# Two residual layers of 512 tokens: modulation loads two steps ahead, x merged tile by tile, and the gating layer's closing product in five pieces

## The chip, the core and the metric

One core of a Trainium2 chip runs one program. The metric is the device time of one execution in microseconds (us). The engines are TensorE (PE: matrix products into PSUM), VectorE (DVE), ScalarE (ACT), GpSimd (POOL) and SyncE (SP), whose queue issues nearly all DMA transfers. Each engine takes its instructions in its own order and waits on semaphores.

## What is computed

A sequence of 512 tokens with 1024 channels goes through two layers. In each layer a token mixer and a dense MLP follow one another, both normalised and modulated by a conditioning vector c, with gates on the way back into x:

```
mod = silu(c) @ ada_w[i] + ada_b[i]          # six vectors of 1024: sh1, sc1, g1, sh2, sc2, g2
h = rms_norm(x, norm_mix[i]) * (1 + sc1) + sh1
x = x + g1 * mixer(h)                        # layer 0: chunked attention, layer 1: spatial gating
h = rms_norm(x, norm_ffn[i]) * (1 + sc2) + sh2
x = x + g2 * (relu(h @ ffn_w1[i]) ** 2 @ ffn_w2[i])

spatial gating: u, v = split(gelu(h @ w_in))         # 3072 columns each
                (u * (W_s rms_norm(v) + b)) @ w_out  # w_out: 3072 x 1024
```

## The kernel before

Everything is float32. Each operand of a product is split into a rounded part (a ScalarE copy) and a rest (a VectorE subtraction), and each product is three TensorE products. Tokens lie in four tiles of 128 rows (t = 0 to 3). On-chip memory is 49 buffers of 4 KB per partition (`NSLOT`), handed out first in, first out by `SL`; a new tile waits until the last user of its buffer is done. The order of instructions on each engine is planned ahead by a list scheduler with a cost model, from the program's order and the dependences. Between `in_order()` and `any_order()` TensorE's order is the written one. `tc.issue_after(ins)` ties what is issued inside it, on the engine of `ins`, behind `ins`.

**Modulation.** For each of the 12 modulation vectors the 1024 x 1024 matrix is read in eight loads of 512 KB; each is multiplied by a column of silu(c) and added up on VectorE (`ada_acc`, L204 and L206), and then either transposed into columns (`ada_columns`) or, for the gates, spread over all rows (`ada_rows`, which also loads the bias row). So a vector is nine steps: one load and its sum each, and a closing one. Ten vectors wait in the queue `bgq` as 90 steps; `bg(n)` takes n of them at set places of the other stages. A step issues its load and uses it at once.

**Layer 0.** Attention head by head; then `ffn(0)`. The MLP's hidden blocks (8 blocks of 512 columns) are "up" steps; each quarter of the second product ("down") is seven block products over sums and differences of blocks (`seven`, Strassen's scheme), which are interleaved with the ups by `steps += [u] + downs[i - 1:i]`. `Run` loads six steps ahead and splits operands three steps ahead. A `Sum` gathers the results (`put`, L489). The last quarter is done plainly by `project_last`: tile by tile, two column halves of 512 each, with the row norm of a finished tile (`rows`) and the transposes of the tile before it (`cols`) in between. x itself has been stored to DRAM (`xs`); `merge(t)` reloads it and computes y * g + x (L798, L799) before the tile's last products are added by `add_residual` (L404: product with the gate, L405: addition to x).

**Layer 1.** The gating half v: two column blocks directly (`gate_tile`, with `bg`), four by the seven-product scheme. Then six column blocks of u (`u_block`), each of four tiles: product, gelu, the gating product, transposes and the split into operands `aTs`. The closing product with `w_out` is cut along the column blocks: `b_down([0])` after block 1, `b_down([1])` after block 2, and after block 5 `b_down([2, 3])` and, in written order, `b_down([4, 5])`. All but the last go through `project`, which multiplies each result with the gate and adds it to x, reloaded whole after block 1. Then `ffn(1)`.

In the functions printed here, those lines matter most: 191 to 209 (step), 266 to 270 (`bg`), 407 to 452 (`project`, `project_last`), 763 to 812 (the steps of the MLP and its end) and 1412 to 1441.

Of the kernel before, what the change touches and what calls it, by code (L numbers as in the profile page):

```python
# [9 lines left out]
F32 = mybir.dt.float32  # L10
# [3 lines left out]
ALU = mybir.AluOpType  # L14
# [38 lines left out]
def trunk_kernel(  # L53
# [37 lines left out]
    def bank():  # L91
        return PS.get([P, 512], F32)
# [82 lines left out]
    def raw_tile(shape):  # L175

        t, i = SL.get(shape, F32)
        return t, lambda: SL.free(i)
# [6 lines left out]
    def ada_acc(l, ms, c0, n, box):  # L185


        nm = len(ms)
        kl = D // n // nm

        def step(k0):
            if k0 == 0:
                box["acc"], box["id"] = SL.get([P, nm * n], F32)
            acc = box["acc"]
            raw, done = raw_tile([P, kl, nm * n])
            src = ada_w[l].rearrange("(p k) (m j) -> p k m j", p=P, m=6)[:, k0:k0 + kl, ms[0]:ms[-1] + 1, c0:c0 + n]
            for k in range(kl if nm > 1 else 0):
                SP.dma_start(raw[:, k, :].rearrange("p (m j) -> p m j", m=nm), src[:, k])
            if nm == 1:
                SP.dma_start(raw, src[:, :, 0, :])  # L200
            for k in range(k0, k0 + kl):
                r, ck = raw[:, k - k0, :], cs[:, k:k + 1]
                if k == 0:
                    V.tensor_scalar(acc, r, ck, None, ALU.mult)  # L204
                else:
                    V.scalar_tensor_tensor(acc, r, ck, acc, ALU.mult, ALU.add)  # L206
            done()

        return [lambda k=k: step(k) for k in range(0, KD, kl)]

    def ada_columns(l, m, box):

# [15 lines left out]
                V.tensor_tensor(r, r, vecT[:, gcol:gcol + 4], ALU.mult)  # L228
        SL.free(box["id"])

    def ada_rows(l, m, box):

        acc = box["acc"]
        raw, done = raw_tile([P, D])
        SP.dma_start(
            raw,
            bass.AP(tensor=ada_b.tensor, offset=ada_b.offset + l * 6 * D + m * D, ap=[[0, P], [1, D]]),
        )
        gt, gi = SL.get([P, D], F32)
        (ah, i0), (al, i1) = SL.get([P, D], F32R), SL.get([P, D], F32R)  # L240
        A.copy(ah, acc)
        V.tensor_tensor(al, acc, f32(ah), ALU.subtract)
        SL.free(i0, i1)
        for hf in range(2):
            sl = slice(hf * 512, hf * 512 + 512)
            ps, pi = bank()
            mm(ps, ones, ah[:, sl], True, False)
            mm(ps, ones, al[:, sl], False, True)
            V.tensor_tensor(gt[:, sl], ps, raw[:, sl], ALU.add)
            PS.free(pi)  # L250
        done()
        gbc[l, m] = (gt, gi)
        SL.free(box["id"])

    def ada_mod(l, m):
        box = {}
        end = (lambda: ada_rows(l, m, box)) if m in (2, 5) else (lambda: ada_columns(l, m, box))
        return ada_acc(l, (m,), 0, D, box) + [end]

    mark = [None]  # L260
# [1 line left out]
    def behind():  # L262

        return tc.issue_after(mark[0].ins) if mark[0] is not None else nullcontext()

    def bg(n):
        with behind():
            for _ in range(n):
                if bgq:
                    bgq.popleft()()  # L270

    region = []

# [130 lines left out]
        V.tensor_tensor(tt, ps, g[:, sl], ALU.mult)  # L404
        V.tensor_tensor(xt[t][:, sl], xt[t][:, sl], tt, ALU.add)  # L405

    def project(actT, src, g):
        for hf in range(2):
            w, ids = wload(src[:, hf * 512:hf * 512 + 512], len(actT))
            for t in range(NT):  # L410
                ps, pi = bank()
                gemm_tok(actT, w, t, ps)
                add_residual(t, hf * 512, ps, g)
                PS.free(pi)
            SL.free(*ids)

    ahead = {}

    def store(t, c0, n):
# [2 lines left out]
    def project_last(actT, src, g, rows, cols=None, after=None, merge=None, spent=None):  # L422


        n = len(actT)
        ws = [wload(src[:, hf * 512:hf * 512 + 512], n) for hf in range(2)]
        if after is not None:
            ahead["w"] = after()
        for t in range(NT):
            if merge is not None:  # L430
                merge(t)
            for hf in range(2):
                w = ws[hf][0]
                nc_ = 256 if cols is None and (t, hf) == (NT - 1, 1) else 512
                for c0 in range(0, 512, nc_):
                    ps, pi = bank()
                    if hf == 1 and t > 0 and cols is not None:
                        gemm_tok(actT, w[:n // 2], t, ps, 0, n - 1)
                        cols(t - 1)
                        gemm_tok(actT, w[n // 2:], t, ps, n // 2, n - 1)  # L440
                    else:
                        gemm_tok(actT, w, t, ps[:, 0:nc_], part=slice(c0, c0 + nc_))
                    add_residual(t, hf * 512 + c0, ps[:, 0:nc_], g)
                    PS.free(pi)
                    if cols is None:
                        store(t, hf * 512 + c0, nc_)
                if t == NT - 1:
                    SL.free(*ws[hf][1])
            if spent is not None:
                spent(t)  # L450
            if cols is not None:
                rows(t)
# [25 lines left out]
    class Sum:  # L478


        def __init__(self):
            self.y, self.ids, self.seen = {}, {}, set()

        def put(self, t, hf, ps):
            if t not in self.y:
# [8 lines left out]
    class Spent:  # L494
# [33 lines left out]
        def done(self, m):  # L528
            self.op.pop(m).free()
# [166 lines left out]
    def ffn(l, norm, rows, cols, after, bgn):  # L696
# [65 lines left out]
        steps = []  # L762
        for q in range(3):
            ups, downs = up_steps(2 * q + 2) + up_steps(2 * q + 3), down_steps(q)
            for i, u in enumerate(ups):
                steps += [u] + downs[i - 1:i]
        run = Run(steps, 3, 3)
        for hf in range(2):
            rng = slice(hf * 256, hf * 256 + 256)
# [20 lines left out]
        up_done(1)  # L790
        run.go()
        g = gbc[l, 5][0]
        def merge(t):

            xt[t], xid[t] = y.y[t], y.ids[t]
            raw, done = raw_tile([P, D])
            SP.dma_start(raw, xs[t])
            V.tensor_tensor(xt[t], xt[t], g, ALU.mult)  # L798
            V.tensor_tensor(xt[t], xt[t], raw, ALU.add)  # L799
            done()  # L800

        in_order()
        parts = {b: Split(t, [P, 4, 256]) for b, (t, _) in quarters(3).items()}
        for b in (6, 7):
# [2 lines left out]
        def spent(t):  # L807
            if t % 2:
                for j in range(2):
                    parts[t // 2, j].free()  # L810

        project_last(plain(parts), ffn_w2[l][3072:4096, :], g, rows, cols, after, merge, spent)


# [86 lines left out]
    def stage_load(ci):  # L901
        c0, k0 = ci * cw, ci * nk
        box = {}
        if ci == 0:
            shift_first(cw)
        for f in ada_acc(0, (1,) if ci == 0 else (0, 1), c0, cw, box):
            f()
        w, ids = wload(a_w_in[0][:, 0:512], nk, k0)
        first_ids.extend(ids)
        w2 = wload_half(a_w_in[0][:, 512:768], k0, nk, V)  # L910
        state[ci] = box, w, w2
# [368 lines left out]
    def gate_tile(cb, t, w):  # L1280

        if cb not in vv:
            vv[cb] = [SL.get([P, 2, 512], F32) for _ in range(2)]
        ps, pi = bank()
        gemm_tok(kept.rows(), w, t, ps)
        bg(((0, 0, 1, 1), (1, 2, 2, 2))[cb][t])
        dst = vv[cb][t // 2][0][:, t % 2, :]
        A.activation(dst, ps, AF.Gelu)
        PS.free(pi)
        tt = tp.tile([P, 512], F32, tag="tt", name="vq")  # L1290
        A.activation(tt, dst, AF.Square, accum_out=vss[:, t, cb:cb + 1])
# [10 lines left out]
    def gate_rows(t):  # L1302
        norm.rows(t)
        if t == 2:
            with tc.issue_after(normed[0].ins):
                kept.half(0)

    ffn(0, mid, gate_rows, norm.cols, lambda: gate_load(0), [3] * 9)
    close(0, 5)
    xs = dp.tile([NT, P, D], F32, name="xsg")  # L1310
    for t in range(NT):
        SP.dma_start(xs[t], xt[t])
        SL.free(xid[t])
    ws = [ahead.pop("w")]
    for t in range(2):
        gate_tile(0, t, ws[0][0])
# [40 lines left out]
    V.tensor_scalar(vr, rsqrt_m2(vs4, NT, SGH), -0.5, None, ALU.mult)  # L1357

    aTs = {}

    def u_block(cb):
        w, ids = u_ahead.pop() if u_ahead else wload(b_w_in[0][:, cb * 512:(cb + 1) * 512], KD)
# [5 lines left out]
        for t in range(NT):  # L1368
# [33 lines left out]
                V.tensor_tensor(lo[:, :, cols], src, f32(hi[:, :, cols]), ALU.subtract)  # L1402
            PS.free(pi)
            SL.free(ui)
            bg((0, 0, 1, 1, 1, 2)[cb])
        SL.free(*ids)
        SL.free(*[i for _, i in vv[cb]])
        aTs[cb] = (tiles, tids)

    last = Norm(1, 3)  # L1410

    def b_down(blocks):
        tiles = [p for b in blocks for p in aTs[b][0]]
        src = b_w_out[0][blocks[0] * 512:(blocks[-1] + 1) * 512, :]
        if 5 in blocks:
            in_order()
            project_last(split_of(tiles), src, gbc[1, 2][0], last.rows, last.cols, lambda: up_ahead(1))
        else:
            project(split_of(tiles), src, gbc[1, 2][0])
        for b in blocks:  # L1420
            for i, j in aTs[b][1]:
                SL.free(i, j)

    u_block(0)
    u_block(1)
    for t in range(NT):
        xt[t], xid[t] = SL.get([P, D], F32)
        SP.dma_start(xt[t], xs[t])
    b_down([0])
    u_block(2)  # L1430
    b_down([1])
    u_block(3)
    u_block(4)
    u_block(5)
    kept.free()
    SL.free(*[i for _, i in wsT])
    b_down([2, 3])
    b_down([4, 5])
    close(1, 2)

    ffn(1, last, None, None, None, [1] * 11)
    any_order()

# [29 lines left out]
```

## Time and profile before

| | |
|---|---|
| median of 3 runs | 1446.78 us (1440.88 to 1448.47) |
| the profiled execution | 1446.44 us |
| its span, first to last instruction | 1444.7 us |
| TensorE products (PE) busy | 1394.3 us, 97% of the span |
| TensorE weight loads (PEld) | 1192.4 us, 83% |
| VectorE (DVE) | 1028.9 us, 71% |
| ScalarE (ACT) | 703.5 us, 49% |
| DMA | 208.92 MB, mean 145 GB/s |

A busy share is an average over stages. Idle time of an engine in a stretch, and what ended it, is read from the stretches and waits further down. PEclk there is the clock granted to TensorE, as a share of 2.4 GHz.

### The profile page before, as it was taken

The numbers are of one execution on the slowest core, as the hardware profiler recorded it, in microseconds if no ns is written. First come the engines' busy times: TensorE is split into PE (matmuls) and PEld (weight loads), VectorE is DVE, ScalarE is ACT, GpSimd is POOL, SyncE is SP. The second block draws the span as 40 slices with busy tenths as digits, with TensorE's granted clock in tenths as the row PEclk, the third lists the DMA queues.
The fourth block names the chain that finished last, engine by engine and source line by source line (L and its number), as shares of the span: only waits on it lengthen the run. The fifth ranks groups of instructions, "written<-read, shape, count | busy, mean of one in ns | idle before, by whom it ended". The sixth has DMA issues, their size and how long they took to land.

```text
span 1444.7 us, 18877 instructions
## 1 busy us (share of the span) xinstructions
PE 1394.3 (97%) x7186; PEld 1192.4 (83%) x7186; DVE 1028.9 (71%) x1509; ACT 703.5 (49%) x1220; POOL 11.1 (1%) x34
## 2 busy tenths in 40 slices
PE   6989889899999999999999999999999999999998
PEld 5879889779888888878878888887889988888877
DVE  6677899667667878865697656868567476867772
ACT  4436667655454544546477532334236355454520
POOL 0000000000000000000000000000000000000000
PEclk9999999899999999999999999999999999999999
DMA  9736664556145263236332343346326225243141
GB/s 332 243 120 174 199 179 129 180 183 227 59 160 190 88 221 103 97 134 231 134 117 88 110 138 123 111 151 206 131 103 247 74 73 160 89 131 102 44 151 53
DMA packets 95458, 208.92 MB, mean 145 GB/s; under 512 B 7808, under 2 KB 25608, under 8 KB 95368
## 3 DMA queue, kind: packets, MB, share of 16 engines
q1 hardware_dynamic: 95184, 207.66, 44.1%
q8 instruction: 56, 0.92, 0.3%
q14 instruction: 34, 0.28, 0.1%
q10 hardware_dynamic: 184, 0.07, 0.0%
HBM read 190.92 MB, written 8.39 MB: 138 GB/s over the span
## 4 chain that ended last, share of the span: by engine, by line
PE 85%; DMA 7%; DVE 5%; ACT 2%; issue 1%; SPq 0%; ACTq 0%; DVEq 0%
PE p L95 81%; DMA s<-in_ada_w 3%; DMA s<-in_ffn_w 1%; DMA s<-in_a_w_in 1%; DVE s L386 1%; DVE s L206 1%; DVE s L473 1%; PE p L1396 1%; ACT s L385 1%; PE p L1092 1%; PE p L312 0%; PE p L1003 0%; DMA vecs<-in_norm_ffn 0%; DMA s<-in_b_w_out 0%; DMA s<-in_x 0%
## 5 line engine op out<-in xcount | busy, mean ns | idle before, releaser
L95 PE MATMUL p<-s,s 128*128 128x512 f32 (+2 forms) x6568 | 1335.5, 363 | 26.4 <-DVE s L473 6.3
L95 PEld LDWEIGHTS p<-s,s 128*128 128x128 f32 x6568 | 1118.2, 191 | 216.1 <-DVE s L473 7.6
L473 DVE TENSOR_TENSOR s<-s,s 128x1024 fp32r<-128x1024 f32 x234 | 281.6, 1221 | 104.8 <-ACT s L472 48.3
L472 ACT CAST s<-s 128x1024 fp32r<-128x1024 f32 x234 | 241.0, 1050 | 180.4 <-PE p L95 99.0
L385 ACT CAST s<-s 128x1024 fp32r<-128x1024 f32 x102 | 106.2, 1050 | 145.1 <-DMA s<-in_b_w_in 30.8
L386 DVE TENSOR_TENSOR s<-s,s 128x1024 fp32r<-128x1024 f32 x102 | 123.6, 1221 | 61.5 <-ACT s L385 55.2
L206 DVE SCALAR_TENSOR_TENSOR s<-s,cs,s 128x1024 f32<-128x1024 f32 (+2 forms) x98 | 108.8, 1110 | 41.4 <-DMA s<-in_ada_w 40.3
L603 DVE TENSOR_TENSOR s<-s,s 128x1024 f32<-128x1024 f32 x64 | 77.7, 1221 | 23.7 <-DMA s<-in_ffn_w 23.1
L711 ACT ACTIVATE r<-p 128x512 f32<-128x512 f32 x64 | 38.1, 595 | 96.7 <-PE p L95 96.6
L404 DVE TENSOR_TENSOR tr<-p,s 128x512 f32<-128x512 f32 (+1 forms) x57 | 38.3, 678 | 54.5 <-PE p L95 54.5
L489 DVE TENSOR_TENSOR s<-p,s 128x512 f32<-128x512 f32 x80 | 54.2, 686 | 18.6 <-PE p L95 18.0
L717 ACT ACTIVATE s<-r 128x256 f32<-128x256 f32 (+1 forms) x112 | 44.9, 442 | 1.0
L301 ACT ACTIVATE s<-s 128x512 f32<-128x512 f32 x32 | 20.2, 631 | 40.7 <-DVE s L405 36.6
L405 DVE TENSOR_TENSOR s<-s,tr 128x512 f32<-128x512 f32 (+1 forms) x57 | 38.4, 680 | 1.1
L1059 ACT ACTIVATE s<-s,nm 128x384 f32<-128x384 f32 (+3 forms) x64 | 35.7, 559 | 6.6 <-DVE nm L1054 4.8
L1054 DVE CUSTOM_DVE_ANT_0 s<-p,s 128x384 f32<-128x384 f32 (+3 forms) x64 | 28.8, 485 | 8.3 <-PE p L95 8.1
L502 DVE TENSOR_TENSOR s<-s,s 128x1024 f32<-128x1024 f32 x28 | 33.5, 1218 | 0.1
L1373 ACT ACTIVATE s<-p 128x512 f32<-128x512 f32 x24 | 14.4, 599 | 39.2 <-PE p L95 38.9
L1401 ACT CAST s<-p 128x256 fp32r<-128x256 f32 x48 | 17.4, 372 | 28.2 <-PE p L1396 22.9
L1402 DVE TENSOR_TENSOR s<-p,s 128x256 fp32r<-128x256 f32 x48 | 19.9, 419 | 14.5 <-ACT s L1401 14.4
L1097 DVE TENSOR_TENSOR s<-p,s 128x512 fp32r<-128x512 f32 (+3 forms) x64 | 29.2, 483 | 0.9 <-ACT s L1096 0.8
L1096 ACT CAST s<-p 128x512 fp32r<-128x512 f32 (+3 forms) x64 | 24.9, 430 | 9.6 <-PE p L1092 9.3
(129 smaller groups left out, 661.0 us busy)
## 6 DMA issues: line engine op xcount, KB each, us to landing
s<-in_ffn_w SPq DMA_DIRECT2D x128, 512.0 KB, 4.4
s<-in_ada_w SPq DMA_DIRECT2D x84, 512.0 KB, 5.0
s<-in_b_w_in SPq DMA_DIRECT2D x48, 512.0 KB, 4.6
s<-in_b_w_out SPq DMA_DIRECT2D x24, 512.0 KB, 5.0
s<-in_a_w_in SPq DMA_DIRECT2D x22, 512.0 KB, 6.1
s<-s SPq DMA_DIRECT2D x64, 128.0 KB, 3.3
s<-in_ada_w SPq DMA_DIRECT2D x24, 256.0 KB, 6.6
s<-in_x SPq DMA_DIRECT2D x8, 512.0 KB, 6.3
```

Of the source, the lines that this page charges most:

```text
L95: T.matmul(ps, lhsT, rhs, start=start, stop=stop, skip_group_check=more)
L206: V.scalar_tensor_tensor(acc, r, ck, acc, ALU.mult, ALU.add)
L385: A.copy(hi, raw)
L386: engs[len(ids) // 2 % len(engs)].tensor_tensor(lo, raw, f32(hi), ALU.subtract)
L404: V.tensor_tensor(tt, ps, g[:, sl], ALU.mult)
L405: V.tensor_tensor(xt[t][:, sl], xt[t][:, sl], tt, ALU.add)
L472: A.copy(self.hi, raw)
L473: mark[0] = V.tensor_tensor(self.lo, raw, f32(self.hi), ALU.subtract)
L489: V.tensor_tensor(dst, ps, dst, ALU.add)
L603: V.tensor_tensor(x[0], y_[0], z[0], ALU.subtract)
L711: A.activation(r, ps, AF.Relu)
L717: A.activation(d, v, AF.Square)
```

## The change

- A modulation step becomes a pair, load and use. `bg` keeps `lead` loads in flight ahead of the use (0 in the attention stage, 2 from layer 0's MLP on) and never takes the queue below `keep`, a limit set for each stage. The gate tiles take one step each and the last of them two; the column blocks 1 to 5 take one per tile. A load's buffer is taken before that of the sum.
- The merge of x moves into `Sum`. Merge of tile 0 is issued right after the operand splits of the last quarter and tied behind the last of them; those of the later tiles are tied behind the row norm last issued. The gating layer uses the same merge: its pieces are summed ungated in a `Sum`, and x is reloaded tile by tile at the end.
- The closing product is in five pieces, [0], [1], [2], [3], [4, 5], with pieces 0 to 3 after column blocks 1 to 4. The first half of the last piece's weights is loaded at the second tile of column block 5.
- In the third quarter of each MLP the downs come one step later.

```diff
-        def step(k0):
-            if k0 == 0:
-                box["acc"], box["id"] = SL.get([P, nm * n], F32)
-            acc = box["acc"]
-            raw, done = raw_tile([P, kl, nm * n])
+        def load(k0):
+            box[k0] = raw, done = raw_tile([P, kl, nm * n])
...
+        def use(k0):
+            if k0 == 0:
+                box["acc"], box["id"] = SL.get([P, nm * n], F32)
+            acc = box["acc"]
+            raw, done = box.pop(k0)
...
+    bgl = deque()
+    lead, keep = [0], [63]
+
     def bg(n):
-        with behind():
-            for _ in range(n):
-                if bgq:
-                    bgq.popleft()()
+        for _ in range(min(n, len(bgl) + len(bgq) - keep[0])):
+            while len(bgq) > keep[0] and len(bgl) <= lead[0]:
+                load, use = bgq.popleft()
+                load()
+                bgl.append(use)
+            with behind():
+                bgl.popleft()()
...
-        ws = [wload(src[:, hf * 512:hf * 512 + 512], n) for hf in range(2)]
+        ws = [ahead.pop(hf) if hf in ahead else wload(src[:, hf * 512:hf * 512 + 512], n) for hf in range(2)]
...
             if merge is not None:
-                merge(t)
+                with tc.issue_after(normed[0].ins) if t else nullcontext():
+                    merge(t)
...
+        def merge(self, xs, g):          # in Sum
+            merged = set()
+            def merge(t):
+                if t in merged:
+                    return
+                merged.add(t)
+                xt[t], xid[t] = self.y[t], self.ids[t]
+                raw, done = raw_tile([P, D])
+                SP.dma_start(raw, xs[t])
+                V.tensor_tensor(xt[t], xt[t], g, ALU.mult)
+                V.tensor_tensor(xt[t], xt[t], raw, ALU.add)
+                done()
+            return merge
...
+            late = 2 if q == 2 else 1
             for i, u in enumerate(ups):
-                steps += [u] + downs[i - 1:i]
+                steps += [u] + (downs[i - late:i - late + 1] if i >= late else [])
+            steps += downs[8 - late:]
...
+        with tc.issue_after(mark[0].ins):          # in ffn, after the operand splits
+            merge = y.merge(xs, g)
+            merge(0)
         project_last(plain(parts), ffn_w2[l][3072:4096, :], g, rows, cols, after, merge, spent)
...
-        bg(((0, 0, 1, 1), (1, 2, 2, 2))[cb][t])
+        bg(1 + ((cb, t) == (1, 3)))
...
+    lead[0], keep[0] = 2, 36
     ffn(0, mid, gate_rows, norm.cols, lambda: gate_load(0), [3] * 9)
...
+    keep[0] = 27          # before the gate tiles; 9 before the column blocks, 0 before ffn(1)
...
-            bg((0, 0, 1, 1, 1, 2)[cb])
+            bg(1 if cb else 0)
+            if (cb, t) == (5, 1):
+                ahead[0] = wload(b_w_out[0][2048:3072, 0:512], KD)
...
-            project_last(split_of(tiles), src, gbc[1, 2][0], last.rows, last.cols, lambda: up_ahead(1))
+            g = gbc[1, 2][0]
+            project_last(split_of(tiles), src, g, last.rows, last.cols, lambda: up_ahead(1), y.merge(xs, g))
         else:
-            project(split_of(tiles), src, gbc[1, 2][0])
+            act = split_of(tiles)
+            for hf in range(2):
+                w, ids = wload(src[:, hf * 512:hf * 512 + 512], len(act))
+                for t in range(NT):
+                    ps, pi = bank()
+                    gemm_tok(act, w, t, ps)
+                    y.put(t, hf, ps)
+                    PS.free(pi)
+                SL.free(*ids)
...
-    for t in range(NT):
-        xt[t], xid[t] = SL.get([P, D], F32)
-        SP.dma_start(xt[t], xs[t])
     b_down([0])
     u_block(2)
     b_down([1])
     u_block(3)
+    b_down([2])
     u_block(4)
+    b_down([3])
     u_block(5)
...
-    b_down([2, 3])
     b_down([4, 5])
```

## Rows read from the trace of the kernel before

**Rows 1.** Stretches: length, busy us by engine, granted clock, DMA share, GB/s.

```profile
core 0: us, PE busy (x) PEld busy (x) DVE busy (x) ACT busy (x) POOL busy (x), PEclk, DMA share, GB/s
100.00:341.00 241.00, 224.03 (x1523) 205.24 (x1522) 190.05 (x449) 152.30 (x354) 8.74 (x21) 0.96 0.61 187
341.00:626.00 285.00, 285.00 (x1405) 242.17 (x1404) 221.52 (x222) 144.04 (x203) 0.00 (x0) 1.00 0.41 134
626.00:642.00 16.00, 12.59 (x49) 9.89 (x48) 13.98 (x15) 4.45 (x7) 0.00 (x0) 0.89 0.26 91
742.00:1004.00 262.00, 262.00 (x1262) 219.63 (x1261) 187.31 (x276) 118.34 (x201) 0.61 (x2) 1.00 0.40 131
...
420.00:440.00 20.00, 20.00 (x90) 16.57 (x89) 13.30 (x13) 13.26 (x18) 0.00 (x0) 1.00 0.77 265
```

**Rows 2.** TensorE's waits, 341 to 1445 us: total, times, longest, us.

```profile
PE p L95 <- DVE s L473: 6.3, 3, 3.4
PE p L95 <- ACT s L385: 2.1, 1, 2.1
PE p L95 <- ACT s L472: 1.4, 1, 1.4
```

**Rows 3.** Timeline of the first gating products: start, duration, engine, idle before.

```profile
709.65 2.60 DVE L206 SCALAR_TENSOR_TENSOR s<-s,cs,s 128x1024 f32<-128x1024 f32 x2 [11.51 <-DMA s<-in_ada_w]
...
735.38 25.00 PE L95 MATMUL p<-s,s 128*128 128x512 f32 x109 [0.98 <-DVE s L473]
```

**Rows 4.** Windows of 2 us behind two of the stops, as rows 1.

```profile
630.00:632.00 2.00, 1.88 (x7) 1.56 (x8) 2.00 (x4) 2.00 (x3) 0.00 (x0) 0.87 0.68 253
632.00:634.00 2.00, 2.00 (x6) 1.51 (x6) 2.00 (x3) 0.52 (x1) 0.00 (x0) 0.50 0.00 0
634.00:636.00 2.00, 2.00 (x9) 1.60 (x8) 2.00 (x3) 0.00 (x0) 0.00 (x0) 0.78 0.00 0
...
1010.00:1012.00 2.00, 2.00 (x8) 1.38 (x7) 2.00 (x5) 0.00 (x0) 0.00 (x0) 0.59 0.91 297
1012.00:1014.00 2.00, 2.00 (x6) 1.53 (x6) 1.18 (x2) 1.26 (x3) 0.00 (x0) 0.56 1.05 392
```

**Rows 5.** Timeline at the end of layer 0's MLP.

```profile
621.64 0.59 ACT L711 ACTIVATE r<-p 128x512 f32<-128x512 f32 x1
...
625.44 1.23 DVE L799 TENSOR_TENSOR s<-s,s 128x1024 f32<-128x1024 f32 x1 [0.41 <-DMA s<-xs]
626.58 1.22 DVE L798 TENSOR_TENSOR s<-s,s 128x1024 f32<-128x1024 f32 x1
...
628.85 1.22 DVE L473 TENSOR_TENSOR s<-s,s 128x1024 fp32r<-128x1024 f32 x1
```

**Rows 6.** Timeline at the end of layer 1's MLP.

```profile
1397.29 1.22 DVE L799 TENSOR_TENSOR s<-s,s 128x1024 f32<-128x1024 f32 x1
1398.42 2.35 DVE L473 TENSOR_TENSOR s<-s,s 128x1024 fp32r<-128x1024 f32 x2
```

**Rows 7.** The page's groups: busy us, mean ns of one, idle before.

```profile
L385 ACT CAST s<-s 128x1024 fp32r<-128x1024 f32 x102 | 106.2, 1050 | 145.1 <-DMA s<-in_b_w_in 30.8
L404 DVE TENSOR_TENSOR tr<-p,s 128x512 f32<-128x512 f32 (+1 forms) x57 | 38.3, 678 | 54.5 <-PE p L95 54.5
L489 DVE TENSOR_TENSOR s<-p,s 128x512 f32<-128x512 f32 x80 | 54.2, 686 | 18.6 <-PE p L95 18.0
```

**Rows 8.** Timeline at the end of the last column block.

```profile
1005.95 1.10 PE L95 MATMUL p<-s,s 128*128 128x128 f32 x6
...
1007.70 0.59 ACT L1373 ACTIVATE s<-p 128x512 f32<-128x512 f32 x1
...
1009.40 0.87 DVE L1391 SCALAR_TENSOR_TENSOR s<-p,bsT,s 128x128 f32<-128x128 f32 x2
```

**Rows 9.** The page's DMA issues: count, size, us to landing.

```profile
s<-in_b_w_out SPq DMA_DIRECT2D x24, 512.0 KB, 5.0
```

**Rows 10.** Waits of SP's queue, 341 to 700 us: total, times, longest, us.

```profile
SPq L684 <- PE p L95: 74.2, 9, 20.2
```

More of the change, by code (lines that the diff above doesn't have):

```diff
@@ L207, in step @@
             done()
-        return [lambda k=k: step(k) for k in range(0, KD, kl)]
+        return [(lambda k=k: load(k), lambda k=k: use(k)) for k in range(0, KD, kl)]
     def ada_columns(l, m, box):
@@ L229, in ada_columns, with ada_bias @@
         SL.free(box["id"])
-    def ada_rows(l, m, box):
-        acc = box["acc"]
-        raw, done = raw_tile([P, D])
+    def ada_bias(l, m, box):
+        box["bias"] = raw, done = raw_tile([P, D])
         SP.dma_start(
@@ L238, in ada_rows @@
         )
+    def ada_rows(l, m, box):
+        acc = box["acc"]
+        raw, done = box["bias"]
         gt, gi = SL.get([P, D], F32)
@@ L256, in ada_mod @@
         box = {}
-        end = (lambda: ada_rows(l, m, box)) if m in (2, 5) else (lambda: ada_columns(l, m, box))
+        if m in (2, 5):
+            end = (lambda: ada_bias(l, m, box), lambda: ada_rows(l, m, box))
+        else:
+            end = (lambda: None, lambda: ada_columns(l, m, box))
         return ada_acc(l, (m,), 0, D, box) + [end]
@@ L405, in add_residual @@
         V.tensor_tensor(xt[t][:, sl], xt[t][:, sl], tt, ALU.add)
-    def project(actT, src, g):
-        for hf in range(2):
-            w, ids = wload(src[:, hf * 512:hf * 512 + 512], len(actT))
-            for t in range(NT):
[L411 to L415, printed above, removed]
     ahead = {}
@@ L792, in ffn @@
         g = gbc[l, 5][0]
[L793 to L800, printed above, removed]
         in_order()
@@ L905, in stage_load @@
             shift_first(cw)
-        for f in ada_acc(0, (1,) if ci == 0 else (0, 1), c0, cw, box):
-            f()
+        for load, use in ada_acc(0, (1,) if ci == 0 else (0, 1), c0, cw, box):
+            load()
+            use()
         w, ids = wload(a_w_in[0][:, 0:512], nk, k0)
@@ L1359, in trunk_kernel @@
     aTs = {}
+    keep[0] = 9
     def u_block(cb):
@@ L1410, in trunk_kernel @@
     last = Norm(1, 3)
+    y = Sum()
     def b_down(blocks):
@@ L1425, in trunk_kernel @@
     u_block(1)
-    for t in range(NT):
-        xt[t], xid[t] = SL.get([P, D], F32)
-        SP.dma_start(xt[t], xs[t])
     b_down([0])
@@ L1436, in trunk_kernel @@
     SL.free(*[i for _, i in wsT])
-    b_down([2, 3])
     b_down([4, 5])
     close(1, 2)
+    keep[0] = 0
     ffn(1, last, None, None, None, [1] * 11)
```

## Prediction

> **What bounds the kernel now.** Read first the stretches of time, then TensorE's waits, then the order on the engine it waits for. The stretches show where a gain can lie: from 341 us on TensorE is busy without a gap in [rows 1] 341 to 626 and 742 to 1004 (285.00 of 285.00, 262.00 of 262.00), and every tensor product there runs at one pace, 90 matmuls in 20 us, 0.222 us each. The number of matmuls doesn't change, so these stretches can only stay or get worse. TensorE's waits from 341 us to the end are three rows [rows 2], 6.3 + 2.1 + 1.4 = 9.8 us, at four places that belong to four handovers:
>
> - a: layer 0's MLP to its closing product, 3.4 us, for VectorE;
> - b: the gating layer's first products, 1.4 + 0.98 = 2.4 us, for ScalarE and VectorE [rows 2, 3];
> - c: the end of its last column block, 2.1 us, for a weight cast;
> - d: layer 1's MLP to its closing product, 6.3 - 3.4 - 0.98 = 1.9 us.
>
> Behind two of them the clock costs more. After stop a the granted clock falls to 0.50, that is from 2.4 to 1.2 GHz; the missing shares in the three windows from 630 us are 0.13 + 0.50 + 0.22 = 0.85 of 2 us, 1.7 us [rows 4]. After stop c they are 0.41 + 0.44 = 0.85, again 1.7 us. So a costs 5.1, b 2.4, c 3.8, d 1.9: 13.2 us are all that this change can take from the time after 341 us. The profiled execution took 1446.44 us (span 1444.7, 1.7 around it), 0.3 below the median 1446.78; the sum is made against 1446.4.
>
> **The change part by part.**
>
> *Merge moved behind the operand splits, third quarter's products one step later (a, d).* In a, VectorE runs in order, and two merge operations (L799, then L798, 1.22 us each) and a weight split stand before the split L473 that TensorE needs [rows 5]. ScalarE took up the last hidden block at 621.64, so its operands could have been split by about 626; the split came at 628.85. In the changed kernel merge(0) is tied behind the four operand splits, and merge(1) to merge(3) behind the row norm before them. Also, two products of 24 matmuls instead of one follow the last hidden block: 24 x 0.222 = 5.3 us more cover. The stop was 3.4, so even with VectorE's old order the cover is longer: a goes whole, 5.1. What is late next is the second half's weights; the same loads as now, split before 624 us, so nothing. In d the row norm is an old one, so merge(1) to merge(3) aren't held there, and one L799 may still stand before the splits as it does now at 1397.29 [rows 6]; but 5.3 us of cover stand against 1.9. I leave 0.5 of 1.9. The step itself moves no work out: the same instructions in another order.
>
> *Modulation loads two steps ahead (b).* Before stop b VectorE stood still 11.51 us for a modulation transfer, and only then started its L206 at 709.65 [rows 3]; nine modulation steps then fall together with the splits of the two big gating products, until TensorE waits. Now one step goes with each of the eight gate tiles and one more with the last, loaded two ahead. Six of L206 at 1.3 us are then done before 709, 7.8 us of VectorE work against a stop of 2.4. The ends: all of the 2.4 gone, or, if the first load of the stage still waits for a free buffer (the stage begins with none in flight, since the limits drain the lead at each boundary), nothing gained. I take 0.8 left, near the lower end, because the idle time is five times the stop. In layer 0's MLP the same edit takes waits from VectorE, but TensorE has none there: worth nothing.
>
> *Bias row loaded as a step of its own, buffer of a load taken before that of the sum.* The instructions are the same. In the attention stage (100 to 341 us, TensorE 224.03 of 241 us, the only other stretch with room) the number of steps at each call is unchanged (27 in all) and the lead is zero, so only the numbers of two buffers change places. Bounds: one like wait of this stage gained or lost, for which stop a's 3.4 is the nearest row; I take 0 and keep +-3.
>
> *Closing product in five pieces, summed ungated (c).* Pieces 2 and 3 were one product behind the last column block; now each stands between blocks. VectorE loses work: 24 results times two operations (L404, and L405 like it, 0.69 each) become 32: 8 copies on ScalarE and 24 additions like L489 at 0.69 [rows 7]. That is 33.1 against 16.6 us, and in front of the last product stand four merges of 2 x 1.22, 9.8 us. Net 6.7 us less, but VectorE isn't the bound between 742 and 1004, so that is worth nothing. What matters is the last block's end. Before, its tail and the missing weights met; now no free product is left to cover the tail, since the closing one runs in written order. The tail: after the last product come gelu 0.59 and the multiply 0.87, against 1.10 us of six gating matmuls [rows 8]: 0.4 us bare, some 0.5 with handovers. The first half's weights are loaded from the second tile of that block on, with two tiles (about 15 us by the pace) still to go: ready. Of the second half, the last two of four loads need buffers that come free only at the tail's end, T. The first of them is ready at T + 5.0 (landing) + 1.05 + 1.22 = T + 7.3 [rows 7, 9], the next at T + 8.5; TensorE wants them after 24 + 12 matmuls, T + 8.0, and 6 matmuls later, T + 9.3. It fits by 0.7; SP issues in order, and the next MLP's four loads stand near: I take 1.0 late. So 1.5 of c is left, too short for a clock drop like the one after 2.1. Ends: 0.5, or rival 1.
>
> *Merges in front of the gating layer's residual.* New work of 2.44 us per tile behind the previous tile's row norm. Queued behind a waiting merge are the residual additions and the norm of that tile, then TensorE's transposes in the middle of the next tile's second half. A tile gives TensorE 48 x 0.222 = 10.7 us; squares, norm, merge and residual take some 7. Ends 0 and 2.44 for the one tile without a predecessor's cover; I take 1.0.
>
> **Sum:** removed 5.1 + 2.4 + 3.8 + 1.9 = 13.2; left 0 + 0.8 + 1.5 + 0.5 = 2.8; new 1.0. Gain 9.4: 1446.4 - 9.4 = 1437.0.
>
> **Rivals.**
>
> 1. *The second half's weights come late at c.* If their transfers queue behind the next MLP's four (392 GB/s after stop c [rows 4], so 512 KB each take 1.3 us), they land 5.3 later; less the margin 0.7 the stop is 4.6, with the clock 6.3, where the forecast has 1.5. For it: these loads stood under pieces 2 and 3 (192 matmuls x 0.222 = 42.6 us), which have moved. Against: they come first in the program. Time: 1437.0 + 4.8 = 1441.8, within 0.5% of before.
>
> 2. *Slower: too few buffers in layer 0's MLP.* Two modulation tiles more are held through the whole of it, of 49 buffers that a count of the code finds nearly all in use. SP is in order and already waits there for buffers [rows 10] (74.2 us for TensorE's releases at the MLP's own weights); a modulation load that waits for one holds the weights behind it. The Trainium skill (Perfetto Trace Analysis, Optimization Strategy) says that a gap that repeats on the engine that should be saturated can mean that the next tile finds no room. By that rule the 341 to 626 stretch, now without a gap, would get one at each of its nine rounds of modulation; no run here shows it yet. A round that starves TensorE costs what a did, 5.1 with the clock. Two use up the gain; from the fourth it is slower by over 0.5%: 1437.0 + 4 x 5.1 = 1457. Against it: some six buffers come free in each 5.3 us step, so two fewer delay a load by about 2 us, and operands are split three steps, 16 us, ahead.
>
> 3. *Nothing:* the stops move instead of going (the written order and a changed plan of VectorE put other splits last). Time 1446. For it: at each stop VectorE is busy nearly throughout the wait (13.98 of 16 us at a). Against: the extra 5.3 us of cover at a and d hold for any order.
>
> **How the numbers follow.** A measurement of this kernel can tell about 0.5%, 7.2 us: the border is 1439.6 and 1454.0. Forecast 0.60 (its own range 1432 to 1442, with the attention stage's +-3), rival 1 0.20, rival 2 0.14, rival 3 0.06. Of the forecast 0.50 lies under 1439.6. So faster 0.50, same 0.10 + 0.20 + 0.06 = 0.36, slower 0.14. The range from 1430 to 1447 holds the first, second and last case; it leaves out rival 2 and a little at the edges.
>
> **What would show it.** No TensorE wait at a and d, and granted clock 1.00 there; merge operations behind the four splits on VectorE at a. L206 without its 11.5 us wait, and TensorE whole, in the first gating products. At c a wait under 2 us; one over 2 with clock under 0.7 is rival 1. Gaps repeating in layer 0's MLP are rival 2. The forecast is wrong if a or d still stops for more than 1 us, or if the attention stage moved by more than 3 us.

## The result and the profile after

The changed kernel took 1437.3 us (median of 13 runs, 1428.84 to 1440.12) against 1446.78 (13 runs); the ratio is 0.9935, with a 95% interval of 0.9919 to 0.9952. The forecast was 1437.0. The sum was nearly met, but not by the terms that it was made of: one stop went for another reason than foretold, and a new one came in a stage for which the forecast had no term.

The first 341 us differ between the profiled executions by more than the change is worth: the mark below stands at 333.99 us in one of them (e7) and at 343.25 in another (e10), and it moves also where the instructions up to it are the same (last section). So each profile is read from that mark on: the transposes of the last token tile at about 340 us. Here are that mark, the transposes of the last tile in layer 0's closing product, and those in the gating layer's, from TensorE's timeline (start, duration, engine, line), first of the kernel before, then of the changed one.

```profile
340.44 1.03 PE L312 MATMUL p<-ident,s 128*128 128x128 f32 x8
...
685.86 1.03 PE L363 MATMUL p<-ident,s 128*128 128x128 f32 x8
...
1113.31 1.03 PE L312 MATMUL p<-ident,s 128*128 128x128 f32 x8
```

```profile
340.42 1.03 PE L329 MATMUL p<-ident,s 128*128 128x128 f32 x8
...
680.51 1.03 PE L380 MATMUL p<-ident,s 128*128 128x128 f32 x8
...
1106.67 1.06 PE L329 MATMUL p<-ident,s 128*128 128x128 f32 x8
```

From mark to mark the change saves 345.42 - 340.09 = 5.33 us, then 427.45 - 426.16 = 1.29, and from the last mark to the ends of the spans (1444.7 and 1436.1) 331.39 - 329.43 = 1.96: 8.6 us, all of the difference of the spans. Ahead of the first mark the two executions differ by 0.02 us; as far as that stage moves between executions, this is chance.

TensorE's waits from 341 us to the end, in the changed kernel (total, times, longest), against [rows 2]:

```profile
PE p L95 <- ACT s L402: 1.8, 1, 1.8
PE p L95 <- DVE s L403: 1.6, 2, 0.9
```

Instead of 9.8 us of waiting there are 3.4, and none of it at a, b or d. The stretches (columns as [rows 1]) say the same: the one behind the MLP, 12.59 of 16 us busy before, is full at full clock, the MLP still has no gap, and only one stretch of the column blocks has one.

```profile
341.00:626.00 285.00, 285.00 (x1405) 242.24 (x1403) 214.76 (x217) 146.30 (x203) 0.00 (x0) 1.00 0.40 131
626.00:642.00 16.00, 16.00 (x73) 13.24 (x72) 14.80 (x20) 4.81 (x8) 0.00 (x0) 1.00 0.38 137
...
896.00:908.00 12.00, 9.50 (x36) 7.09 (x35) 9.13 (x14) 6.57 (x9) 0.00 (x0) 0.86 0.59 204
908.00:1056.00 148.00, 148.00 (x712) 123.80 (x711) 96.39 (x143) 49.31 (x76) 0.00 (x0) 1.00 0.42 136
```

At a, the order on VectorE is the foretold one, against [rows 5]: both splits that TensorE needs first (L481) stand ahead of the first merge operation (L503).

```profile
620.79 2.35 DVE L481 TENSOR_TENSOR s<-s,s 128x1024 fp32r<-128x1024 f32 x2
623.07 1.22 DVE L503 TENSOR_TENSOR s<-s,s 128x1024 f32<-128x1024 f32 x1
```

At d the splits are done at 1386 us, a merge's product with the gate (L503) follows right behind them, and the first L504, its addition, comes at 1392.34, against [rows 6], where an addition (L799) stands ahead of the splits:

```profile
1384.86 1.22 DVE L481 TENSOR_TENSOR s<-s,s 128x1024 fp32r<-128x1024 f32 x1
...
1392.34 2.35 DVE L504 TENSOR_TENSOR s<-s,s 128x1024 f32<-128x1024 f32 x2
```

At b, six of the modulation sums (L209) are done before 709 us, and the 11.51 us wait of [rows 3] has become 2.72:

```profile
693.20 2.59 DVE L209 SCALAR_TENSOR_TENSOR s<-s,cs,s 128x1024 f32<-128x1024 f32 x2
...
697.04 2.60 DVE L209 SCALAR_TENSOR_TENSOR s<-s,cs,s 128x1024 f32<-128x1024 f32 x2
...
706.20 2.60 DVE L209 SCALAR_TENSOR_TENSOR s<-s,cs,s 128x1024 f32<-128x1024 f32 x2 [2.72 <-DMA s<-in_ada_w]
```

The new stop, e, stands at 900 us: column block 2 has just ended (blocks and pieces are counted from 0) and piece [1] of the closing product begins, 96 matmuls from 902.18 on. The kernel before has the same piece at the same place and no wait there ([rows 1], 742 to 1004). On TensorE, and with the granted clock behind it:

```profile
902.18 1.21 PE L95 MATMUL p<-s,s 128*128 128x512 f32 x4 [1.81 <-ACT s L402]
904.09 11.21 PE L95 MATMUL p<-s,s 128*128 128x512 f32 x41 [0.69 <-DVE s L403]
...
1056.99 10.96 PE L95 MATMUL p<-s,s 128*128 128x512 f32 x47 [0.92 <-DVE s L403]
```

```profile
904.00:906.00 2.00, 1.91 (x5) 1.55 (x6) 1.22 (x3) 1.93 (x3) 0.00 (x0) 0.62 0.14 54
906.00:908.00 2.00, 2.00 (x6) 1.55 (x5) 1.33 (x3) 0.95 (x2) 0.00 (x0) 0.52 0.02 4
```

1.81 + 0.69 of wait and (0.38 + 0.48) x 2 = 1.7 by the clock make 4.2 us. The last wait, 0.92 at 1057, is what is left at the end of the column blocks, where c was; behind it no clock is lost. SP's queue ahead of e: a modulation load, the next one 13 us later, then at once a row of gains, and the first weights of piece [1] at 886.95.

```profile
867.85 0.34 SPq L197 DMA_DIRECT2D s<-in_ada_w  x1
...
880.88 0.33 SPq L197 DMA_DIRECT2D s<-in_ada_w  x1
881.26 0.42 SPq L1389 DMA_DIRECT2D gain<-in_b_v_gain  x1
...
886.95 2.25 SPq L399 DMA_DIRECT2D s<-in_b_w_out  x2
```

Those 13 us are one wait at the head of the queue for a buffer that TensorE's products hold; behind it the weights wait 5.3 us more for a buffer that the transposes hold (waits of SP's queue, 870 to 905 us):

```profile
SPq L197 <- PE p L95: 12.6, 1, 12.6
SPq L399 <- PE p L1421: 10.0, 2, 5.3
```

### The profile page after: what moved, and what is told of

Its sections match the earlier page's. It is cut to its first block, busy times and chain, and to the rows that moved or that the text cites. A ratio compares the mean times of both kernels' runs of the same rounds, so it can differ in the third digit from the quotient of the medians.

```text
span 1436.1 us, 18871 instructions
## 1 busy us (share of the span) xinstructions
PE 1391.4 (97%) x7186; PEld 1191.1 (83%) x7186; DVE 1020.0 (71%) x1493; ACT 709.1 (49%) x1228; POOL 10.0 (1%) x34
## 4 chain that ended last, share of the span: by engine, by line
PE 77%; DMA 2%; DVE 1%; ACT 1%; issue 0%; SPq 0%; DVEq 0%; ACTq 0%
PE p L95 76%; DMA s<-in_ffn_w 1%; DVE s L403 1%; PE p L1421 1%; PE p L329 1%; DMA s<-in_b_w_in 0%; ACT s L480 0%; DMA s<-in_b_w_out 0%; PE p L222 0%; PE p L380 0%; DVE s L481 0%; ACT s L402 0%; ACT tt L333 0%; DVE s L1119 0%; DVE s L1143 0%
## 5 line engine op out<-in xcount | busy, mean ns | idle before, releaser
L481 DVE TENSOR_TENSOR s<-s,s 128x1024 fp32r<-128x1024 f32 x234 | 280.3, 1219 | 113.0 <-ACT s L480 53.7
L480 ACT CAST s<-s 128x1024 fp32r<-128x1024 f32 x234 | 241.6, 1051 | 174.5 <-PE p L95 109.4
L403 DVE TENSOR_TENSOR s<-s,s 128x1024 fp32r<-128x1024 f32 x102 | 123.3, 1221 | 70.5 <-ACT s L402 59.3
L209 DVE SCALAR_TENSOR_TENSOR s<-s,cs,s 128x1024 f32<-128x1024 f32 (+2 forms) x98 | 108.6, 1109 | 12.9 <-DMA s<-in_ada_w 11.8
L514 DVE TENSOR_TENSOR s<-p,s 128x512 f32<-128x512 f32 x104 | 70.3, 684 | 34.6 <-PE p L95 33.4
L421 DVE TENSOR_TENSOR tr<-p,s 128x512 f32<-128x512 f32 (+1 forms) x33 | 21.9, 670 | 30.3 <-PE p L95 30.0
L1402 ACT CAST s<-s 128x512 fp32r<-128x512 f32 x24 | 14.5, 620 | 44.2 <-DVE s L1400 25.6
L1114 PE MATMUL p<-ident,s 128*128 128x128 f32 x160 | 24.0, 276 | 5.8 <-ACT sq L1195 3.2
```

Of the source, the lines that this page charges most:

```text
L403: engs[len(ids) // 2 % len(engs)].tensor_tensor(lo, raw, f32(hi), ALU.subtract)
L480: A.copy(self.hi, raw)
L481: mark[0] = V.tensor_tensor(self.lo, raw, f32(self.hi), ALU.subtract)
L514: V.tensor_tensor(dst, ps, dst, ALU.add)
```

## Experiments

"Rest" is the span from the mark at 340 us to its end, in the one profiled execution of each kernel. "Waits" is TensorE's waiting in it, "clock" the time that the lower clock cost there: the missing share of the granted clock, summed over windows of 2 us. Ratios are to the kernel before, from all runs, with 95% intervals.

| run | made from | rest, us | waits | clock | ratio |
|---|---|---|---|---|---|
| the kernel before | | 1104.3 | 9.8 | 3.4 | 1 |
| the change | | 1095.7 | 3.4 | 1.7 | 0.9935 (0.9919 to 0.9952) |
| e1, downs in old place | changed | 1098.4 | 5.8 | 1.7 | 0.9948 (0.9929 to 0.9968) |
| e2, merges not tied | changed | 1095.6 | 3.7 | 1.7 | 0.9946 (0.9930 to 0.9961) |
| e6, e1 and e2 | changed | 1103.4 | 9.6 | 3.4 | 0.9969 (0.9948 to 0.9991) |
| e7, downs later | before | 1097.3 | 5.3 | 1.7 | 0.9962 (0.9942 to 0.9982) |
| e8, steps spread over gate tiles | before | 1100.4 | 7.8 | 1.7 | 0.9985 (0.9971 to 0.9999) |
| e5, no load ahead anywhere | changed | 1093.5 | 3.1 | 0 | 0.9914 (0.9884 to 0.9945) |
| e3, none in the column blocks | changed | 1092.4 | 2.4 | 0 | 0.9909 (0.9888 to 0.9930) |
| e12, one in the column blocks | changed | 1089.9 | 0.2 | 0 | 0.9904 (0.9884 to 0.9924) |
| e4, four pieces | changed | 1097.5 | 3.6 | 3.4 | 0.9953 (0.9930 to 0.9977) |
| e10, four pieces | e3 | 1096.2 | 3.7 | 1.7 | 0.9938 (0.9919 to 0.9958) |
| e9, block steps counted as changed | before | 1105.9 | 10.7 | 3.4 | 1.0026 (1.0004 to 1.0049) |
| e11, ungated sums | before | 1109.9 | 12.8 | 6.8 | 1.0038 (1.0022 to 1.0053) |

In all fourteen the rest less its waits and its clock loss is 1089.7 to 1091.8 us. So TensorE's stops and the clock behind them make up the differences. A rest is read from one execution, and 1.7 us between two rests can be the clock alone.

### Tie or cover (e1, e2, e6, e7)

```diff
-            late = 2 if q == 2 else 1     # e1
+            late = 1
```

> The changed kernel with the third quarter's down products back in their old place (late = 1 in all quarters); merges still tied behind the operand splits. Theory 1 (the tie alone takes VectorE's delay away: the split that TensorE needs could be ready about 0.3 us after TensorE ran out at stop a): at a at most 1 us of wait and no clock drop, at d 1 to 2 us because merges 1 to 3 are not tied there; total 1 to 3 us above the changed kernel. Rival (it is the 5.3 us of cover that removes both): stops of 2 us or more at both, with the clock drop of 1.7 at a; total 5 to 7 us above the changed kernel.

At a no wait at all, at d 2.68 us and no clock drop; the rest is 2.7 longer. So at a the tie is enough. At d it isn't, as merges 1 to 3 are not held there: two L503 of merges stand on VectorE ahead of the weight split L403 that TensorE waits for (TensorE's and VectorE's timelines of e1).

```profile
1396.01 37.10 PE L95 MATMUL p<-s,s 128*128 128x512 f32 x185 [2.68 <-DVE s L403]
```

```profile
1391.87 2.35 DVE L503 TENSOR_TENSOR s<-s,s 128x1024 f32<-128x1024 f32 x2
...
1394.74 1.22 DVE L403 TENSOR_TENSOR s<-s,s 128x1024 fp32r<-128x1024 f32 x1
```

```diff
-                with tc.issue_after(normed[0].ins) if t else nullcontext():    # e2
-                    merge(t)
+                merge(t)
...
-        with tc.issue_after(mark[0].ins):
-            merge = y.merge(xs, g)
-            merge(0)
+        merge = y.merge(xs, g)
```

> The changed kernel without any tie of the merges and with merge 0 at its old place behind the weight loads; down products still one step later. Theory 1 (5.3 us of cover against stops of 3.4 and 1.9 suffices in any order of VectorE): no TensorE wait over 0.5 us at a and d; total within 1 us of the changed kernel. Rival (the order on VectorE decides): a stop of 2 us or more at a, total 2 to 5 us above.

No wait at a or d (all that is left is 2.3 + 0.7 us at e and 0.6 at the end of the column blocks), and the rest is the changed kernel's: the cover, the product more that TensorE has ready behind the last hidden block, suffices alone, in the free order of VectorE. e6 takes both edits together.

> The changed kernel with neither the ties of the merges nor the later down products; modulation and closing product as changed. Theory 5 (at a, tie and cover are each enough alone): with neither, stop a is back with 2 us or more and its clock drop, and d with 2 to 3: total 5 to 8 us above the changed kernel. Rival (the modulation steps, which no longer stand on VectorE there, cleared a): a under 0.5 us, d 2 to 3; total 2 to 3 us above.

Both stops are back as in [rows 2], 3.31 and 2.05 us, the rest is 7.7 longer (by the ratios the loss is about 5 us), and on VectorE two merge operations (L503, L502) stand again ahead of the split (L480). That settles theory 5; the modulation steps had no part in a. TensorE and VectorE of e6:

```profile
628.33 17.77 PE L95 MATMUL p<-s,s 128*128 128x512 f32 x70 [3.31 <-DVE s L480]
...
1397.37 40.95 PE L95 MATMUL p<-s,s 128*128 128x512 f32 x202 [2.05 <-DVE s L480]
```

```profile
623.64 1.23 DVE L503 TENSOR_TENSOR s<-s,s 128x1024 f32<-128x1024 f32 x1 [0.30 <-DMA s<-xs]
624.78 1.22 DVE L502 TENSOR_TENSOR s<-s,s 128x1024 f32<-128x1024 f32 x1
...
627.05 1.22 DVE L480 TENSOR_TENSOR s<-s,s 128x1024 fp32r<-128x1024 f32 x1
```

In e7 the later downs stand alone in the kernel before:

```diff
+            late = 2 if q == 2 else 1     # e7
             for i, u in enumerate(ups):
-                steps += [u] + downs[i - 1:i]
+                steps += [u] + (downs[i - late:i - late + 1] if i >= late else [])
+            steps += downs[8 - late:]
```

> The kernel before with one edit: the third quarter's down products one step later. Theory 5: stops a and d go, 5.1 + 1.9, total 6 to 7 us below the kernel before; b and c stay at 2.4 and 2.1. Rival (VectorE's order refills the cover with other splits): a or d stays at 1.5 us or more, total at most 3 us below.

a and d are gone, b (2.32 + 0.44) and c (2.61) stay, the rest is 7.0 shorter, the foretold sum of a and d. That it is met so closely is in part chance: b and c are 0.9 us longer than before, and the clock fell at b, not at c. This small edit is worth most of the change: ratio 0.9962, against 0.9935 for the whole.

```profile
722.38 1.97 PE L95 MATMUL p<-s,s 128*128 128x512 f32 x5 [2.32 <-ACT s L472]
724.78 65.00 PE L95 MATMUL p<-s,s 128*128 128x512 f32 x282 [0.44 <-DVE s L473]
1000.37 0.73 PE L95 MATMUL p<-s,s 128*128 128x512 f32 x2 [2.61 <-ACT s L385]
```

### Spread or lead (e8, e5, e3, e12)

```diff
-        bg(((0, 0, 1, 1), (1, 2, 2, 2))[cb][t])     # e8, in gate_tile
+        bg(1 + ((cb, t) == (1, 3)))
```

> The kernel before with one edit: at the gate tiles one modulation step each and two at the last, instead of 0, 0, 1, 1, 1, 2, 2, 2; no load ahead. Theory 4: stop b (1.4 + 1.0) is under 0.5 us, total 2 to 3 us below the kernel before, with a, c and d as they were. Rival (without loads ahead VectorE waits for the transfers as before): b stays at 1.5 us or more, total within 1 us.

b is gone without any load ahead, and a, c and d are still there. The rest is 3.9 shorter: 2.4 of b, and most of the remainder is that behind this c, of 2.49 us, the clock did not fall, as it did before. TensorE of e8:

```profile
627.04 17.79 PE L95 MATMUL p<-s,s 128*128 128x512 f32 x70 [3.21 <-DVE s L473]
1004.53 0.73 PE L95 MATMUL p<-s,s 128*128 128x512 f32 x2 [2.49 <-ACT s L385]
1393.13 40.95 PE L95 MATMUL p<-s,s 128*128 128x512 f32 x202 [2.04 <-DVE s L473]
```

```diff
-    lead[0], keep[0] = 2, 36     # e5
+    lead[0], keep[0] = 0, 36
```

> The changed kernel with every modulation load issued at its use (lead 0 from layer 0's MLP on); the steps stay spread as in the change. Theory 4 (stop b went because the steps are spread over the eight gate tiles, and the lead is worth nothing in the MLP and costs the 4.2 us at 900 us): no TensorE wait over 0.5 us in the first gating products, none at 900 us; total 4 to 6 us below the changed kernel, within 1.5 of e3. Rival (the lead removed b): a stop of 1.5 us or more in the first gating products, 2 to 3 us above e3.

The stop at 900 us is gone, and a wait of 1.41 is back in the first gating products. So theory 4 holds for the spread (e8), but inside the changed kernel the lead is worth something there as well; its rival's 1.5 us was nearly met. TensorE of e5:

```profile
727.49 64.89 PE L95 MATMUL p<-s,s 128*128 128x512 f32 x284 [1.41 <-ACT s L480]
```

```diff
-    keep[0] = 9                  # e3, ahead of the column blocks
+    lead[0], keep[0] = 0, 9
...
-    keep[0] = 0
+    lead[0], keep[0] = 2, 0
```

> The changed kernel with modulation loads issued at their use again in the gating layer's column blocks alone (lead 0 there, 2 elsewhere). The changed kernel has a new stop there, 1.8 + 0.7 us at 900 us with a clock drop of 1.7, 4.2 in all. Theory 2 (a modulation load waits 12.6 us at the head of SP's queue for a buffer and holds the closing product's weights behind it): the stop goes, total 3 to 4 us below the changed kernel. Rival (the weights of piece 2 are late because their own buffers come free late, with or without modulation loads): the stop stays at 2 us or more, total within 1 us.

e is gone and the rest 3.3 shorter. TensorE's waits in e3 from 341 us on:

```profile
PE p L329 <- DVE s L320: 1.3, 1, 1.3
PE p L95 <- DVE s L403: 1.1, 2, 0.8
```

e12 sets `lead[0], keep[0] = 1, 9` at the same place.

> The changed kernel with one modulation load ahead instead of two in the gating layer's column blocks (lead 1 there, 2 elsewhere). Theory 2 (the load that stands furthest ahead waits longest for its buffer and holds the weights behind it): with one ahead SP's wait is shorter, the stop at 900 us is under 1 us with no clock drop, and the time behind the attention stage is within 1 us of e3. Rival (any load ahead there costs the stop): 2 us or more with the clock drop, within 1 us of the changed kernel.

The stop is gone, and the rest is 2.5 shorter still than in e3, the shortest of all: behind the attention stage TensorE waits once, 0.2 us. But SP's queue still waits long for a modulation load, 10.3 us at one time, and no stop follows. TensorE's and SP's waits of e12 (SP from 855 to 895 us):

```profile
PE p L95 <- DVE s L403: 0.2, 1, 0.2
```

```profile
SPq L197 <- PE p L95: 15.9, 2, 10.3
```

So two loads ahead make e, as theory 2 says; but that the wait at the head of the queue does it isn't shown. Two tiles held also change which buffers the weights get, and in the changed kernel the weights waited 5.3 us for their own, when the modulation load had already gone. The first weights of piece [1] go out at 886.95 there, at 882.28 in e12 and at 880.69 in e3 (below), with marks at 340.42, 341.44 and 339.69. This points to the weights' own buffers, which e3's rival names, but freed late because of the lead; no run changes one of the two without the other.

```profile
880.69 8.86 SPq L399 DMA_DIRECT2D s<-in_b_w_out  x3
```

### What removed c (e4, e10, e9, e11)

```diff
-            if (cb, t) == (5, 1):                 # e4
-                ahead[0] = wload(b_w_out[0][2048:3072, 0:512], KD)
...
-    b_down([2])
     u_block(4)
-    b_down([3])
     u_block(5)
...
+    b_down([2, 3])
     b_down([4, 5])
```

> The changed kernel with pieces 2 and 3 as one product after the last column block, as before, and without the early weight load; sums still ungated. Theory 3 (five pieces remove stop c, 3.8 us with the clock, and bring the stop at 900 us, 4.2): the stop at 900 us goes, one of 2 us with a clock drop comes back at the last column block's end; total within 1 us of the changed kernel. Rival (the early and the ungated sums alone had removed c): no stop at either place, total 3 to 5 us below.

Theory 3 fell on both counts: e stays (2.19 + 0.68), and at the place of c, the last tile of column block 5, TensorE doesn't wait at all (0.45 and 0.28 us stand earlier, at 982 and 987, at the turn from block 4 to block 5). That e stays was bound to come out so. The expectations of e3 and e4 take e to be at piece 2, but it is at piece [1], which e4 leaves as it is; up to 927 us the two kernels run the same instructions in the same order on every engine. So five pieces do not bring e, and c stays away without them; whether they would remove c under the old counts was not run. The 1.8 us by which e4's rest is longer are not the price of four pieces either: e waits 0.4 us longer and loses 3.4 us by the clock instead of 1.7, both ahead of all that the edit touches. Windows of e4 behind e:

```profile
902.00:904.00 2.00, 1.27 (x4) 0.67 (x4) 1.96 (x3) 0.42 (x2) 0.00 (x0) 0.80 0.96 367
904.00:906.00 2.00, 1.85 (x4) 1.49 (x5) 1.22 (x3) 1.88 (x3) 0.00 (x0) 0.50 0.03 9
906.00:908.00 2.00, 2.00 (x6) 1.59 (x5) 1.45 (x3) 1.00 (x2) 0.00 (x0) 0.50 0.02 4
908.00:910.00 2.00, 2.00 (x6) 1.52 (x6) 1.18 (x2) 0.00 (x0) 0.00 (x0) 0.50 0.00 0
```

e10 makes the same edit in e3.

> The kernel of e3 (no load ahead in the column blocks) with pieces 2 and 3 as one product after the last block and no early weight load. Theory 7 (the cut into five pieces is itself worth about the 1.8 us by which e4 is longer than the changed kernel behind the attention stage): 1 to 2.5 us more than e3 there, no stop at 900 us. Rival (it is worth nothing once no load holds SP's queue): within 0.5 us of e3.

3.7 us more than e3, with a new stop of 2.19 us and its clock drop at 969 us, behind column block 3, where e3 has piece [2]: where no load runs ahead, five pieces are worth more than theory 7 had it. e9 shows how.

```diff
-            bg((0, 0, 1, 1, 1, 2)[cb])                                      # e9, in u_block
+            bg(0 if cb == 0 or (cb, t) in ((5, 2), (5, 3)) else 1)
```

> The kernel before with one edit: in the gating layer's column blocks the modulation steps as the changed kernel counts them (one per tile from block 1 to the second tile of block 5, 18 in all, instead of 0, 0, 1, 1, 1, 2 per tile, 20 in all); no load ahead. Theory 6 (stop c went because two modulation steps per tile no longer fall on the last block): c under 1 us with no clock drop, about 3 us less than the kernel before behind the attention stage; a, b, d as before. Rival (c went because the sums are ungated and x is merged late): c stays at 2 us or more, behind the attention stage within 1 us of before.

At the place of c no wait is left (0.84 and 0.69 us with no clock drop stand earlier, at 980 and 989): the counts removed it, as theory 6 says. One doubt is left here, that the new stop some 40 us ahead gave c's loads time. But e4 has the same counts, nothing over 0.45 us in the 100 us ahead of that place, and no c either. The rest is 1.6 longer than before, not 3 shorter, since the stop at 969 us is here too. On VectorE a modulation sum (L206) waits 4.58 us for its transfer, the multiply (L1391) stands behind it, and TensorE's transposes wait for that. VectorE and TensorE of e9:

```profile
965.97 2.60 DVE L206 SCALAR_TENSOR_TENSOR s<-s,cs,s 128x1024 f32<-128x1024 f32 x2 [4.58 <-DMA s<-in_ada_w]
968.49 0.87 DVE L1391 SCALAR_TENSOR_TENSOR s<-p,bsT,s 128x256 f32<-128x256 f32 x2
```

```profile
969.02 0.83 PE L1396 MATMUL p<-ident,s 128*128 128x128 f32 x4 [2.17 <-DVE s L1391]
```

With loads ahead (e4), or with pieces of the closing product at hand as free work (e3), that stop stays away.

e11 is e4 with the modulation counts, the lead (0), the down products and the MLP's merges of the kernel before; what is left of the change are in the main the ungated sums and the merge by tiles, here untied.

```diff
-    lead[0], keep[0] = 2, 36                      # e11: e4, and
+    lead[0], keep[0] = 0, 36
...
-        bg(1 + ((cb, t) == (1, 3)))
+        bg(((0, 0, 1, 1), (1, 2, 2, 2))[cb][t])
...
-            bg(1 if cb else 0)
+            bg((0, 0, 1, 1, 1, 2)[cb])
```

> The kernel before with one edit: the gating layer's four pieces summed ungated and x merged tile by tile in the last one, all else as before (modulation counts, no load ahead, down products and MLP merges in their old places). Theory 6: c stays at 2 us or more, behind the attention stage within 1 us of before. Rival (the ungated sums removed c): c under 1 us, about 3 us less than before there.

c stays, 2.39 us, so the sums did not remove it. And the rest is 5.6 longer than before: a wait of 2.63 us for a row norm in the last product comes on top, and the clock fell behind it and behind d, 1.7 us each.

```profile
1006.35 1.22 PE L95 MATMUL p<-s,s 128*128 128x512 f32 x2 [2.39 <-ACT s L402]
...
1073.77 1.32 PE L329 MATMUL p<-ident,s 128*128 128x128 f32 x8 [2.63 <-ACT s L318]
```

## Why the prediction was right, and where it wasn't

- **a, 5.1 foretold, 5.33 measured.** Right in size and mechanism: the cover alone removes it, as the forecast says (e2, e7). What it had not seen is that the tie alone does so too (e1), so that a was removed twice over (e6).
- **b, 1.6 foretold of 2.4, all of it measured.** Right: the steps spread over the tiles (e8). The part of the lead was not separated in the forecast; in the changed kernel it takes away a wait of 1.41 us (e5).
- **c, 2.3 foretold.** The step that failed is "What matters is the last block's end": that the cut into five pieces decides there. c went by the modulation counts (e9, e4, e11), which the forecast does not weigh there, and its 3.8 us contained a clock drop that comes and goes (last section). 0.92 are left where 1.5 were foretold, the right size for the wrong reason.
- **The new stop e, 4.2, foretold nowhere.** The part on the modulation loads prices two loads ahead in the gate tiles and in the MLP; for the column blocks, where the same lead holds, it has no term and gives no reason. Rival 2 comes nearest, with buffers that the lead holds and weights that come late for it, but put them in layer 0's MLP, where TensorE stays without a gap. What came is one gap, at the stage where blocks, pieces and modulation share the buffers, and one load fewer ahead removes it (e12). The Trainium skill (Perfetto Trace Analysis, Optimization Strategy) says that the same gap repeating on the engine that should be saturated can mean that there is no room for the next tile. No gap repeats here; this one came alone.
- **Merges in front of the residual, 1.0 foretold.** No wait of TensorE for them in the changed kernel; without the other edits, and untied, they come with more (e11, 2.63 us).
- **d, 1.4 foretold, 1.96 measured.** Right: the cover, not the tie (e1, e7).
- **The sum.** Between the second and third mark the forecast had 1.6 + 2.3 - 1.0 = 2.9 us of gain and 1.29 were measured; the stops give 2.4 + 3.8 - 4.2 - 0.9 = 1.1. The errors cancelled: b (0.8), c (0.6) and the merges (1.0) came out 2.4 better than foretold, a and d 0.8, and e took 4.2 back. That 1437.0 was hit to 0.3 is luck within the foretold 1432 to 1442. One of the forecast's signs of being wrong could not serve: the stage up to 341 us moves by more than 3 us between executions of the same instructions (last section).

The shortest rest is that of the changed kernel with one load ahead in the column blocks (e12), 5.8 us shorter than the changed kernel's; its time is 1432.08 us (median of 6 runs), ratio 0.9904 (0.9884 to 0.9924). By the ratios it can't be told from e3 or e5, and its interval still touches the changed kernel's.

## What to carry to other kernels

Where the bounding engine stops only at handovers, one step more of its own work between the last producer and the first consumer is the cheap cure; here it held in each order of VectorE that was run (the change, e2, e7). Loads ahead are not free: they hold buffers, and two ahead made a stop in the column blocks that one or none did not. So their depth is set, and tried, stage by stage. Edits that come together are to be undone one at a time: here two removed the same stop, and one that looked like the cure of another was not needed for it.

## What was not expected of the hardware

- The clock drop behind a stop is no fixed price. It fell behind 2.13 us at c in the kernel before [rows 4], but not behind 2.49 at the same place in e8, 2.61 in e7, nor behind 2.68 at d in e1; and it fell behind e's 1.81 + 0.69, behind 2.17 in e9, and at b in e7 (2.32 + 0.44). Up to e the changed kernel and e4 run the same instructions, and e cost 1.7 us by the clock in one and 3.4 in the other. So a stop of 2 to 3 us cost 0, 1.7 or 3.4 us more, and part of that changes from execution to execution; with one trace of each kernel the runs don't show whether an edit elsewhere has a part in it.
- The stage up to 340 us differs between executions with the same instructions in it. e7, e8 and e9 run the instructions of the kernel before there, in the same order on every engine, and their marks stand at 333.99, 337.55 and 335.90, against 340.44. The mark of e7:

```profile
333.99 1.03 PE L312 MATMUL p<-ident,s 128*128 128x128 f32 x8
```

That is 6.5 us, three quarters of what the change is worth. One kernel's times spread like that too, the changed one's over 11.3 us. A single total time would have misjudged most of these runs.
